# Twelve gate blocks as six pairs of seven block products ahead of the attention, six conv tiles in PSUM, squares of q and k in one operation

## The chip, the cores and the metric

The kernel runs on one core of one Trainium2 chip. The metric is the device time of one execution in microseconds. A core has TensorE (PE: matmuls, and PEld: the weight loads that run beside them), VectorE (DVE), ScalarE (ACT), GpSimd (POOL) and SyncE (SP, which issues most DMAs). TensorE writes to PSUM, the other engines read it from there.

## The reference

One layer of a decoder on x of 1024 tokens by 1024 channels, in float32:

```python
h = rms_norm(x, attn_norm_w[l])
proj = h @ w_in[l]
q, k, v, u, g = jnp.split(proj, splits, axis=-1)

q = rms_norm(q.reshape(B, S, N_HEADS, 2, HEAD_DIM), q_norm_w[l])
k = rms_norm(k.reshape(B, S, N_HEADS, 2, HEAD_DIM), k_norm_w[l])
...
a = diff_attention(q[0], q[1], k[0], k[1], v, lam, rel_bias)
a = rms_norm(a, subln_w[l]) * (1.0 - lam_init)
y_a = a.reshape(B, S, ATTN_WIDTH) @ w_proj_attn[l]

u_a, u_b = jnp.split(u, 2, axis=-1)
c = causal_depthwise_conv(u_a * jax.nn.sigmoid(u_b), conv_w[l], conv_b[l])
c = jax.nn.silu(layer_norm(c, conv_ln_w[l], conv_ln_b[l]))
y_b = c @ w_proj_conv[l]

g_a, g_b = jnp.split(jax.nn.sigmoid(g + gate_b[l]), 2, axis=-1)
x = x + (g_a * y_a + g_b * y_b) @ w_out[l]

h = rms_norm(x, ffn_norm_w[l])
gt, up = jnp.split(h @ w_gate_up[l], 2, axis=-1)
x = x + (jax.nn.silu(gt) * up) @ w_down[l]
```

`diff_attention` has 8 heads, each with two 64-wide parts of q and k, two causal softmaxes with a relative bias and a 128-wide v; its result is the first softmax minus lambda times the second, applied to v. The convolution is 31 wide over 1024 channels. g has 2048 columns (two gates).

## The kernel before

Every float32 product is made of three matmuls: each operand is split into a high part, rounded to a format that TensorE takes at full rate, and the low rest (`split_hi`, a cast on ScalarE, L120; `split_lo`, a subtraction on VectorE, L125, or on GpSimd, L131), and hi*hi, lo*hi and hi*lo are added (L168 to L170). h is kept transposed, `hT_hi` and `hT_lo`, for the whole input projection.

The output columns of that projection are made in items: V0 to V3 (256 columns of v), Q0 to Q7 (q and k of one head), U0 to U7 (a 128-channel tile of u) and G0 to G15 (a 128-column block of g). A G item (`g_item`) is two groups of 24 matmuls of 512 columns; each group ends in an ACT operation that adds the bias and a store to `g_d`. A Q item is four groups; ACT copies each group out of PSUM and squares it, eight operations with accumulated sums (L783).

U1 to U7 are made as pairs (`u_pair`): the two 128-column halves of a U item and the two halves of the tokens and of the channels form a two by two block product, and seven block products with sums of blocks take the place of eight. One block product is 12 matmuls of 512 columns (`product`, L963), so a pair has 84 where two plain blocks have 96. The sums of h's blocks (`TS`) are made once; those of the weights are made per pair by `prepare`, on GpSimd: four sums (L944 to L947) and the low parts of the splits (L131), while ScalarE makes the high parts. `ahead` is that generator for the next pair, advanced three times during a pair.

The order: an opening with V0 and U0; V1, V2 and the seven u pairs (to about 252 us in the profile); Q0 and V3; the attention, from about 310 to 823 us; the projection of its result (`w_proj_attn`) with the conv's layer norm (`ln_chunks`, `ln_step`) woven in; the conv's projection with the gates; w_out; and the feed-forward part, also by seven block products.

The conv is one DVE operation per tap (L582), 31 entries and a load for each of 8 channel tiles, in a list `bg` that is worked off beside other stages. The accumulators of the first `CONV_PSUM` tiles lie in PSUM and are finished in the first stage (`bg.until` at its end); the others are spread over the attention.

The attention has 64 steps: 8 heads by 8 blocks of 128 queries, `(h, i)`, in the order i = 4, 5, 6, 7, 0, 1, 2, 3 (6, 7, 4, 5, 2, 3, 0, 1 in the last head). A step makes the scores of both halves (`sc`; L1271, L1272) in pieces of up to 512 keys, each read by a DVE operation that adds the bias and keeps the minimum (L1273); ACT makes the exponentials (L1278), DVE combines both halves (L1288). One step later the result is transposed (`pT`, L1310) and split (`ph` by ACT, `pl` by DVE); after every second step it is multiplied with v (`pW`, `weigh`), and two steps later transposed back (`pB`, `back`). The finished head goes to `a_d` and is loaded again (`early`, L1468) and split into `aTh`, `aTl` for the projection.

Between these TensorE works off `fill`: the Q items of the next heads and all G items, in groups, one or none per step by `groups(n)`, and what is left after the last step. How many conv taps a step gets comes from `slack_of(n)`, an estimate of TensorE's and VectorE's time of the step in us.

All engines run their own instructions in order; which instruction stands where is set by the order of the code, by `after(...)` (an instruction is put behind a given one of another stream) and by a scheduler over them.

Of the kernel before, what the change touches and what calls it, by code (L numbers as in the profile page):

```python
# [16 lines left out]
P = 128  # L17
# [40 lines left out]
def kernel(  # L58
# [53 lines left out]
    def nm(s):  # L112
        uid[0] += 1
        return f"{s}_{uid[0]}"
# [9 lines left out]
    def split_lo(dst, src, hi):  # L124
        last_lo[0] = dve.tensor_tensor(dst, src, f32(hi), op=ALU.subtract).ins  # L125
# [244 lines left out]
    def gemm_N(o, halves, shi, slo, i):  # L370
# [24 lines left out]
    last = ["Q0", "V3"]  # L395
    later = [
        ["Q1", "G0", "G1"],
        ["Q2", "G2", "G3"],
        ["Q3", "G4"],
        ["Q4", "G5", "G6"],  # L400
        ["Q5", "G7"],
        ["Q6", "G8", "G9"],
        ["Q7", "G10"],
        ["G11", "G12", "G13", "G14"],
        ["G15"],
    ]

# [9 lines left out]

    for it in ["U0"] + first + last + [x_ for l_ in later for x_ in l_]:
        ws.plan(loads_of(it))
# [136 lines left out]
    us = {}  # L556
    CONV_PSUM = 4
    pcv = []
# [210 lines left out]
    def q_item(h):  # L769
# [3 lines left out]
        for b in (1, 0):  # L773
            raw = qkp.tile([P, 4, 256], F32, tag="qkraw", name=nm("qkraw"), bufs=2)
            ss = sm.tile([P, 16], F32, tag="ss16", name=nm("ss16"))
            for i2 in range(2):
                o = pg()
                for e in range(2):
                    gemm_N(o[:, 256 * e : 256 * (e + 1)], halves, hT_hi, hT_lo, 4 * b + 2 * i2 + e)
                act.copy(raw[:, 2 * i2 : 2 * i2 + 2, :], o[:].rearrange("p (e c) -> p e c", c=256))  # L780
                jk = sm.tile([P, VD], F32, tag="jk", name=nm("jk"), bufs=1)[:, :HD]
                for g in range(8):
                    act.activation(  # L783
                        jk, o[:, g * HD : (g + 1) * HD], AF.Square, accum_out=ss[:, 8 * i2 + g : 8 * i2 + g + 1]
                    )
                if i2 == 0:
                    yield
# [187 lines left out]
    def u_pair(c, A, ahead):  # L975
# [34 lines left out]
        return nxt  # L1010

    def first_stage():

# [3 lines left out]
        yield from opening()  # L1017
        ups = [prepare(win, (U0 + D + c * P, U0 + c * P), st[0], 2, c == 1) for c in range(1, NKT)]

        def weights_ahead():  # L1020
            yield
            ws.ahead = 1
            ws.fetch()
            yield

        for n, _ in enumerate(run(first)):
# [14 lines left out]
            yield  # L1041
        for c in range(1, NKT):
            ahead = ups[c] if c < NKT - 1 else weights_ahead()
            next(ahead)
            A = yield from u_pair(c, A, ahead)
        st_ctx.close()
# [472 lines left out]
    def ln_chunks(sb):  # L1519
# [15 lines left out]
        split_hi(s1h[:], s1[:])  # L1535
        split_lo(s1l[:], s1[:], s1h[:])
        for s_ in (s1h, s1l):
            pe.matmul(mean[:], part[:], s_[:], start=s_ is s1h, stop=s_ is s1l)
# [48 lines left out]

    def ln_step():
        for _ in range(lnp.pop(0)):
            next(lnq, None)  # L1590
# [31 lines left out]
    for c in range(NE):  # L1622
        ya_out(c, o3[c], g3[c])
    ln_step()
    for c in range(NE, NKT):
        w = ws.next()
        ln_step()
        ya_out(c, [gemm_T(w, aT_hi, aT_lo, sb) for sb in range(2)])
    while lnp:
# [362 lines left out]
```

## Time and profile before

| | before |
|---|---|
| median of 3 runs | 1743.23 us (1742.2 to 1744.04) |
| profiled execution | 1742.87 us, span 1741.1 us |
| TensorE, VectorE, ScalarE, GpSimd busy | 1728.2, 1249.4, 856.2, 210.9 us |
| mean granted TensorE clock | 0.999 |

A row of a group of instructions gives the line, the engine, the operation, output and inputs by the program's names, the shape, the count, and behind the bar the busy time in us, the mean of one in ns, the idle time of the engine just before them and what ended it. A row of the timeline gives start and length in us. Matmuls overlap in the records: the time from one start to the next is what one costs. A row of a stretch of time gives its bounds and length, then busy time and count of PE, PEld, DVE, ACT and POOL, the granted clock, the share of the DMA engines and GB/s. A row of DMA issues gives the size of one and the median time from issue to landing.

### The profile page before, as it was taken

To read this page: it belongs to the slowest core of one execution; us is meant where nothing else is said; L and a number is where in the kernel's file an instruction comes from. 1 tells how busy PE (TensorE), PEld (TensorE's weight loads), DVE (VectorE), ACT (ScalarE), POOL (GpSimd) and SP (SyncE) were. 2 spreads that over 40 slices of the span, in tenths; PEclk is the share of its full clock that TensorE was granted. 3 is DMA by queue.
4 is the path that set the end of the run, shared out by engine and by line. 5 is a ranking of instruction groups with operands and counts; after the bars stand their busy time and mean duration, and the time that the engine had idled before them with its cause. 6 is when DMAs were issued, how large, how long until landed. Compare 5 with 4: busy or idle time off the path is not lost.

```text
span 1741.1 us, 25854 instructions
## 1 busy us (share of the span) xinstructions
PE 1728.2 (99%) x9293; PEld 1488.6 (85%) x9293; DVE 1249.4 (72%) x2090; ACT 856.2 (49%) x1950; POOL 210.9 (12%) x199
## 2 busy tenths in 40 slices
PE   9999999999999999999999999999999999999999
PEld 7997889998998999988787888888888888888887
DVE  7575889898987988977787525876676666565554
ACT  5333435767776776756366313633333333333332
POOL 3997851000000000000000000000000000000000
PEclk9999999999999999999999999999999999999999
DMA  6343454234345244343863544235445444597663
GB/s 200 118 129 119 161 177 140 91 107 134 104 110 151 80 119 131 103 140 135 310 208 100 173 157 154 89 99 185 152 152 173 160 151 147 173 369 274 216 219 130
DMA packets 253253, 271.68 MB, mean 156 GB/s; under 512 B 15746, under 2 KB 177602, under 8 KB 253124
## 3 DMA queue, kind: packets, MB, share of 16 engines
q1 hardware_dynamic: 250848, 263.25, 46.7%
q0 software_dynamic: 1840, 5.19, 1.0%
q8 instruction: 73, 1.20, 0.3%
q10 hardware_dynamic: 436, 1.58, 0.2%
q14 instruction: 56, 0.46, 0.1%
HBM read 175.55 MB, written 78.16 MB: 146 GB/s over the span
## 4 chain that ended last, share of the span: by engine, by line
PE 91%; DVE 3%; DMA 2%; ACT 2%; POOL 1%; issue 1%; SPq 0%; POOLq 0%; DVEq 0%
PE acc L963 28%; PE acc L500 12%; PE pg L168 11%; PE pg L170 11%; PE pg L169 11%; PE sc L1272 2%; PE sc L1271 2%; PE pT L1310 2%; PE wo L170 2%; PE wo L169 2%; PE wo L168 2%; DVE acc L582 1%; PE pW L169 1%; PE pW L168 1%; PE pW L170 1%; PE pg L1089 1%
## 5 line engine op out<-in xcount | busy, mean ns | idle before, releaser
L582 DVE SCALAR_TENSOR_TENSOR acc<-u,cw,acc 128x1023 f32<-128x1023 f32 (+14 forms) x240 | 303.5, 1265 | 14.4 <-ACT acc L576 11.9
L168 PE MATMUL pg<-whi,hT_hi 128*128 128x256 f32 x704 | 200.2, 286 | 0.5 <-DVE v L125 0.5
L170 PE MATMUL pg<-whi,hT_lo 128*128 128x256 f32 x704 | 200.1, 285 | 0.0
L169 PE MATMUL pg<-wlo,hT_hi 128*128 128x256 f32 x704 | 199.7, 284 | 0.0
L120 ACT CAST whi<-wraw 128x1024 fp32r<-128x1024 f32 x100 | 105.0, 1052 | 126.4 <-PE wo L170 48.2
L125 DVE TENSOR_TENSOR wlo<-draw,whi 128x1024 fp32r<-128x1024 f32 x75 | 91.8, 1224 | 86.1 <-ACT whi L120 84.4
L125 DVE TENSOR_TENSOR wlo<-wraw,whi 128x1024 fp32r<-128x1024 f32 x85 | 104.9, 1236 | 56.5 <-ACT whi L120 55.9
L120 ACT CAST whi<-draw 128x1024 fp32r<-128x1024 f32 x75 | 79.0, 1053 | 129.6 <-PE acc L500 116.1
L168 PEld LDWEIGHTS pg<-whi,hT_hi 128*128 128x128 f32 x704 | 134.1, 191 | 2.2 <-DVE v L125 0.7
L169 PEld LDWEIGHTS pg<-wlo,hT_hi 128*128 128x128 f32 x704 | 134.4, 191 | 1.9
L170 PEld LDWEIGHTS pg<-whi,hT_lo 128*128 128x128 f32 x704 | 134.3, 191 | 1.7
L500 PE MATMUL acc<-wlo,whi 128*128 128x512 f32 x308 | 120.0, 390 | 0.0
L500 PE MATMUL acc<-whi,wlo 128*128 128x512 f32 x308 | 119.9, 389 | 0.0
L168 PE MATMUL pg<-hT_hi,whi 128*128 128x512 f32 x288 | 114.7, 398 | 0.1
L169 PE MATMUL pg<-hT_lo,whi 128*128 128x512 f32 x288 | 114.2, 397 | 0.0
L170 PE MATMUL pg<-hT_hi,wlo 128*128 128x512 f32 x288 | 113.8, 395 | 0.0
L1278 ACT ACTIVATE E<-E,mn 128x640 f32<-128x640 f32 (+7 forms) x128 | 99.7, 779 | 27.1 <-DVE mn L1273 26.4
L120 ACT CAST whi<-s 128x1024 fp32r<-128x1024 f32 x54 | 56.9, 1053 | 107.3 <-PE acc L963 103.5
L963 PE MATMUL acc<-h_hi,whi 128*128 128x512 f32 x240 | 93.5, 390 | 0.0
L963 PE MATMUL acc<-h_lo,whi 128*128 128x512 f32 x240 | 93.5, 390 | 0.0
L1273 DVE CUSTOM_DVE_ANT_0 E<-sc,tb 128x512 f32<-128x512 f32 (+3 forms) x128 | 74.1, 585 | 26.9 <-PE pT L1310 13.1
L963 PE MATMUL acc<-h_hi,wlo 128*128 128x512 f32 x240 | 90.2, 390 | 0.0
(337 smaller groups left out, 4554.9 us busy)
## 6 DMA issues: line engine op xcount, KB each, us to landing
wraw<-in_w_gate_up_dram SPq DMA_DIRECT2D x44, 512.0 KB, 4.9
wraw<-in_w_in_dram SPq DMA_DIRECT2D x40, 512.0 KB, 4.6
qs<-qs SPq DMA_DIRECT2D x96, 128.0 KB, 2.3
wd<-in_w_down_dram SPq DMA_DIRECT2D x44, 256.0 KB, 3.1
tdT<-wd SPq DMA_DIRECT2D x88, 128.0 KB, 4.7
draw<-sdS SPq DMA_DIRECT2D x44, 256.0 KB, 3.7
draw<-tdT SPq DMA_DIRECT2D x44, 256.0 KB, 4.0
wraw<-in_w_in_dram SPq DMA_DIRECT2D x32, 256.0 KB, 3.3
```

The costliest lines, as they stand in the source:

```text
L120: act.copy(dst, src)
L125: last_lo[0] = dve.tensor_tensor(dst, src, f32(hi), op=ALU.subtract).ins
L168: pe.matmul(o, lh, rh, start=start, stop=False)
L169: pe.matmul(o, lh, rl, start=False, stop=False)
L170: last_mm[0] = pe.matmul(o, ll, rh, start=False, stop=stop).ins
L500: m = pe.matmul(o[s_][i][:], l_[:, ts], r_[:, 512:], start=start and j + y_ == 0, stop=j == n - 1 and y_ == 2, skip_group_check=not start,)
L582: dve.scalar_tensor_tensor(a_, us[c][:, : S - n], cw[:, c, t : t + 1], a_, op0=ALU.mult, op1=ALU.add)
L963: last_mm[0] = pe.matmul(o[:], a_[x_][:, k, :], b_[y_][:, k, :], start=start and k + x_ + y_ == 0, stop=k == 3 and x_ == 1, skip_group_che ...
L1271: pe.matmul(o[:, :w], qh[:, qs], k, start=True, stop=False)
L1272: last_mm[0] = pe.matmul(o[:, :w], ql[:, qs], k, start=False, stop=True).ins
L1273: dve.tensor_tensor_reduce(e[:, ks], o[:, :w], tb[:, S - nk + c0 : S - nk + c0 + w], 1.0, mn[:, j : j + 1] if c0 else 3.0e38, ALU.add, ALU ...
L1278: act.activation(e[:, :nk], e[:, :nk], AF.Exp, bias=mn[:, j : j + 1], scale=-1.0, accum_out=l[:, j : j + 1])
```

## The change

- G0 to G11 are no longer items of `fill`. A new `g_pair` makes two neighbouring gate blocks by seven block products, in the first stage, behind the seven u pairs and prepared like them. Three of its four quarter results get their bias by a DVE operation with the other product (`add`), the fourth by ACT; each is stored to `g_d`.
- `fill` is Q1 to Q7, then G12 to G15: 36 groups in place of 60. Two of them are issued ahead of the first step, each with three entries of `bg`. Then `groups(n)` gives four per head (steps 0, 2, 5 and 7 of a head), and one per step in the last head.
- `CONV_PSUM` is 6: conv tiles 4 and 5 are also finished in the first stage.
- The squares of q and k: one ACT operation of 512 columns and one DVE reduce over groups of 64 take the place of eight ACT operations with sums.
- In the layer norm of the conv the two mean matmuls come one piece later (`yield`), the pieces are counted anew (`ln_both`, `lnp`), and the piece with the first mean is put inside the first group of the third projection block (`ln_amid`).

```diff
-    later = [
-        ["Q1", "G0", "G1"],
...
-        ["G11", "G12", "G13", "G14"],
-        ["G15"],
-    ]
+    NGP = 6
+    later = [f"Q{h}" for h in range(1, H)] + [f"G{c}" for c in range(2 * NGP, 2 * NKT)]
...
-    CONV_PSUM = 4
+    CONV_PSUM = 6
...
-                jk = sm.tile([P, VD], F32, tag="jk", name=nm("jk"), bufs=1)[:, :HD]
-                for g in range(8):
-                    act.activation(
-                        jk, o[:, g * HD : (g + 1) * HD], AF.Square, accum_out=ss[:, 8 * i2 + g : 8 * i2 + g + 1]
-                    )
+                sq = wp.tile([P, 512], F32, tag="sg", name=nm("qsq"), bufs=2)
+                act.activation(sq[:], o[:], AF.Square)
+                dve.tensor_reduce(
+                    ss[:, 8 * i2 : 8 * i2 + 8], sq[:].rearrange("p (g d) -> p g d", d=HD), axis=AX.X, op=ALU.add
+                )
...
+    def g_pair(c, A, ahead):
+
+        B = {(j, l): (hT_hi[:, KH[j], TOK[l]], hT_lo[:, KH[j], TOK[l]]) for j in range(2) for l in range(2)}
+        a, b, c_ = acc(), acc(), acc()
+
+        def add(d, o, l, t_):
+            dve.scalar_tensor_tensor(t_, o[:], pcol("gate_b", d), t_, op0=ALU.add, op1=ALU.add)
+            nc.sync.dma_start(g_d[d][:, TOK[l]], t_)
+
+        product(b, A["11"], B[0, 0], True)
+        p1 = half("p1")
+        act.copy(p1, b[:])
+        product(a, A["12"], B[1, 0], True)
+        add(c, a, 0, p1)
+        nxt = next(ahead, None)
+        yield
+        product(b, A["S2"], TS[2], False)
+        u2 = half("u2")
+        act.copy(u2, b[:])
+        product(c_, A["S1"], TS[1], True)
+        u3 = half("u3")
+        act.copy(u3, c_[:])
+        next(ahead, None)
+        yield
+        product(b, A["S3"], TS[3], False)
+        add(c + 1, b, 1, u3)
+        product(c_, A["S4"], B[1, 1], False)
+        add(c, c_, 1, u2)
+        yield
+        product(b, A["22"], TS[4], False)
+        p2 = half("p1")
+        act.activation(p2, b[:], AF.Identity, bias=pcol("gate_b", c + 1))
+        nc.sync.dma_start(g_d[c + 1][:, TOK[0]], p2)
+        next(ahead, None)
+        yield
+        return nxt
...
-        ups = [prepare(win, (U0 + D + c * P, U0 + c * P), st[0], 2, c == 1) for c in range(1, NKT)]
+        pairs = [(u_pair, c, (U0 + D + c * P, U0 + c * P)) for c in range(1, NKT)]
+        pairs += [(g_pair, 2 * c, (G0 + 2 * c * P, G0 + (2 * c + 1) * P)) for c in range(NGP)]
+        ups = [prepare(win, cols, st[0], 2, z == 0) for z, (_, _, cols) in enumerate(pairs)]
...
-    fill = run(it for l_ in later for it in l_)
-    plan = [sum(4 if it[0] == "Q" else 2 for it in l_) for l_ in later]
+    fill = run(later)
+    for _ in range(2):
+        next(fill)
+        with after(last_of(mybir.EngineType.DVE)):
+            bg.step(3)
...
-        return 0 if plan[n // NT] == 6 and n % NT in (4, 6) or n == len(steps) - 1 else 1
+        return int(n >= len(steps) - NT or n % NT in (0, 2, 5, 7))
...
-        for z in (0, 1, 0, 0, 0, 1, 1, 0, 0, 0, 1, 1, 1, 1):
+        for z in (0, 0, 1, 1, 0, 0, 0, 1, 1, 0, 0, 0, 1, 1, 1, 1):
...
-    lnp = [1, 3, 2, 2, 2, 2, 2, 9]
+    lnp = [1, 1, 4, 2, 2, 2, 2, 9]
...
+    def ln_amid():
+        with after(last_mm[0]):
+            ln_step()
+
     for c in range(NE, NKT):
         w = ws.next()
-        ln_step()
-        ya_out(c, [gemm_T(w, aT_hi, aT_lo, sb) for sb in range(2)])
+        if c > NE:
+            ln_step()
+        ya_out(c, [gemm_T(w, aT_hi, aT_lo, sb, ln_amid if c == NE and not sb else None) for sb in range(2)])
```

TensorE at the end of the attention, before: the last probabilities are transposed (`pT`), weighed (`pW`) and transposed back (`pB`), and a gate group (`pg<-hT`) stands between them and the projection (`pg<-aTh`):

```order
L1310 MATMUL pT_9727<-ident,E_9675 128x128 x2
L1330 MATMUL pB_9787<-ident,ar_9671 128x128 x2
L168 MATMUL pW_9795<-ph_9691,vh_9147 128x256
...
L170 MATMUL pW_9795<-ph_9691,vl_9148 128x256
L168 MATMUL pg_9853<-hT_hi,whi_9454 128x512
...
L1330 MATMUL pB_9820<-ident,ar_9802 128x128 x2
L168 MATMUL pg_9853<-hT_hi,whi_9454 128x512
L169 MATMUL pg_9853<-hT_lo,whi_9454 128x512
L170 MATMUL pg_9853<-hT_hi,wlo_9455 128x512
L168 MATMUL pg_9967<-aTh_9737,whi_9611 128x512
```

The same place after the change:

```order
L1340 MATMUL pT_9621<-ident,E_9553 128x128
L1340 MATMUL pT_9625<-ident,E_9601 128x128 x2
L1360 MATMUL pB_9651<-ident,ar_9597 128x128 x2
L168 MATMUL pW_9659<-ph_9617,vh_9112 128x256
...
L170 MATMUL pW_9659<-ph_9617,vl_9113 128x256
L1360 MATMUL pB_9684<-ident,ar_9666 128x128 x2
L168 MATMUL pg_9801<-aTh_9635,whi_9217 128x512
```

The gate group is gone from between `pW` and the projection; the last matmul on `hT` now stands ahead of the scores of step (7,2)'s second half.

TensorE in head 0 before, from the last score piece of step (0,7) to the first of (0,0): gate matmuls stand between the two.

```order
L1271 MATMUL sc_3521<-ks_0_1_2761,qs_0_1_2774 128x512
L1272 MATMUL sc_3521<-ks_0_1_2761,qs_0_1_2779 128x512
L170 MATMUL pg_3773<-hT_hi,wlo_3185 128x512
L168 MATMUL pg_3837<-hT_hi,whi_3190 128x512
...
L1271 MATMUL sc_3622<-ks_0_0_2940,qs_0_0_2953 128x128
L1272 MATMUL sc_3622<-ks_0_0_2940,qs_0_0_2956 128x128
```

After:

```order
L1301 MATMUL sc_4400<-ks_0_1_3604,qs_0_1_3617 128x512
L1302 MATMUL sc_4400<-ks_0_1_3604,qs_0_1_3622 128x512
L1301 MATMUL sc_4429<-ks_0_0_3771,qs_0_0_3784 128x128
L1302 MATMUL sc_4429<-ks_0_0_3771,qs_0_0_3787 128x128
L169 MATMUL pW_4361<-pl_4245,vh_3980 128x256
```

The scores of (0,0) follow those of (0,7) directly, with the weighing behind them in place of a gate group.

VectorE in head 0 after the change, between two score pieces of step (0,7) and the next ones: conv taps (`acc<-u,cw,acc`) stand between the attention's own operations as before the change.

```order
L1303 ISA E_4395,mn_4383<-sc_4400,tb_3398,mn_4383 128x512
L1303 ISA mn_4383 128x1
L573 SCALAR_TENSOR_TENSOR acc_3474<-u_3090,cw,acc_3474 128x1002
L630 TENSOR_SCALAR t_4341<-t_4341 128x16
L1303 ISA E_4428,mn_4426<-sc_4429,tb_3398 128x128
L1303 ISA mn_4426 128x1
L573 SCALAR_TENSOR_TENSOR acc_3474<-u_3090,cw,acc_3474 128x1001
L1315 RECIPROCAL rl_0_4145<-l_4384 128x2
```

By this order head 0 has 21 taps where 20 stood, and each of the next six heads 3 or 4 where 12 to 15 stood, with four reduces (`ss16<-qsq`) in most of them.

More of the change, by code (lines that the diff above doesn't have):

```diff
@@ L395 @@
     last = ["Q0", "V3"]
-    later = [
-        ["Q1", "G0", "G1"],
[L398 to L403, printed above, removed]
-        ["G11", "G12", "G13", "G14"],
-        ["G15"],
-    ]
+    NGP = 6
+    later = [f"Q{h}" for h in range(1, H)] + [f"G{c}" for c in range(2 * NGP, 2 * NKT)]
     def loads_of(it):
@@ L416, in loads_of @@
         return ld_cols(win, G0 + c * P)
-    for it in ["U0"] + first + last + [x_ for l_ in later for x_ in l_]:
+    for it in ["U0"] + first + last + later:
         ws.plan(loads_of(it))
@@ L1041, in first_stage @@
             yield
-        for c in range(1, NKT):
-            ahead = ups[c] if c < NKT - 1 else weights_ahead()
+        for z, (make, c, _) in enumerate(pairs):
+            ahead = ups[z + 1] if z + 1 < len(pairs) else weights_ahead()
             next(ahead)
-            A = yield from u_pair(c, A, ahead)
+            A = yield from make(c, A, ahead)
         st_ctx.close()
@@ L1536, in ln_chunks @@
         split_lo(s1l[:], s1[:], s1h[:])
+        yield
         for s_ in (s1h, s1l):
```

1 line of the change is left out of this document (removed).

## The prediction

> **What bounds the kernel now.** I read the page's busy shares first, then the chain that ended last, then the attention head by head.
>
> ```profile
> PE 1728.2 (99%) x9293; PEld 1488.6 (85%) x9293; DVE 1249.4 (72%) x2090; ACT 856.2 (49%) x1950; POOL 210.9 (12%) x199
> ...
> PE 91%; DVE 3%; DMA 2%; ACT 2%; POOL 1%; issue 1%; SPq 0%; POOLq 0%; DVEq 0%
> ```
>
> TensorE is busy 99% of the span and is 91% of the chain: fewer matmuls shorten the kernel, as long as no other engine makes TensorE wait. The view by stretches of time asks who could: one row per head, then the tail of attention.
>
> ```profile
> 310.10:375.20 65.10, 65.10 (x436) 59.96 (x436) 60.35 (x124) 42.97 (x140) 0.73 (x4) 1.00 0.28 82
> 375.20:440.80 65.60, 65.48 (x440) 59.71 (x439) 57.09 (x128) 49.57 (x167) 1.44 (x8) 1.00 0.45 129
> 440.80:501.20 60.40, 60.40 (x444) 57.24 (x443) 52.56 (x124) 45.44 (x155) 1.45 (x8) 1.00 0.37 106
> 501.20:565.90 64.70, 64.57 (x430) 58.76 (x429) 52.98 (x122) 47.29 (x153) 1.80 (x10) 1.00 0.45 130
> 565.90:627.60 61.70, 61.48 (x453) 58.22 (x452) 54.44 (x124) 45.19 (x166) 1.09 (x6) 1.00 0.37 104
> 627.60:691.40 63.80, 63.80 (x427) 58.28 (x426) 56.91 (x126) 46.56 (x157) 1.69 (x10) 1.00 0.43 124
> 691.40:754.20 62.80, 62.80 (x416) 57.31 (x416) 53.25 (x122) 47.03 (x160) 1.20 (x7) 1.00 0.37 106
> 754.20:802.80 48.60, 48.60 (x279) 42.15 (x278) 42.66 (x95) 29.48 (x74) 1.45 (x8) 1.00 0.38 114
> 802.80:822.70 19.90, 19.62 (x100) 16.18 (x99) 12.79 (x22) 12.96 (x35) 0.36 (x2) 1.00 0.60 211
> ```
>
> The columns after the length are busy time (and count) of TensorE, its weight loads, VectorE, ScalarE and GpSimd. TensorE never waits, but VectorE has 60.35 us of work in a head of 65.10, and 53 to 57 in the next ones. What separates the two is the gate matmuls that the change takes out.
>
> **The change part by part.** Durations, from the groups and the timeline:
>
> ```profile
> L582 DVE SCALAR_TENSOR_TENSOR acc<-u,cw,acc 128x1023 f32<-128x1023 f32 (+14 forms) x240 | 303.5, 1265 | 14.4 <-ACT acc L576 11.9
> ```
>
> ```profile
> L168 PE MATMUL pg<-hT_hi,whi 128*128 128x512 f32 x248 | 98.7, 398 | 0.1
> L1273 DVE CUSTOM_DVE_ANT_0 E<-sc,tb 128x512 f32<-128x512 f32 x80 | 54.4, 685 | 21.3 <-PE sc L1272 8.6 <-PE pT L1310 8.3 <-PE pg L170 3.4
> L783 ACT ACTIVATE jk<-pg 128x64 f32<-128x64 f32 x224 | 50.5, 225 | 5.0
> L783 ACT ACTIVATION_READ_ACCUMULATOR jk<-pg 128x1 f32 x224 | 44.7, 199 | 0.0
> L125 DVE TENSOR_TENSOR wlo<-wraw,whi 128x1024 fp32r<-128x1024 f32 x30 | 36.5, 1220 | 2.4 <-ACT whi L120 1.8 <-PE pg L170 0.5
> L790 DVE TENSOR_TENSOR qkraw<-qkraw,r 128x1024 f32<-128x1024 f32 x14 | 17.0, 1218 | 0.0
> ```
>
> ```profile
> 228.76 0.39 PE L963 MATMUL acc<-T3h,whi 128*128 128x512 f32 x1
> ...
> 231.49 0.39 PE L963 MATMUL acc<-hT_hi,wlo 128*128 128x512 f32 x1
> ```
>
> Twelve 512-column matmuls lie between the two starts, so one costs (231.49 - 228.76)/12 = 0.227 us of TensorE.
>
> *Matmuls.* Twelve gate blocks of 48 matmuls become six pairs of 84: 576 - 504 = 72 fewer, 72 x 0.227 = 16.3 us gained, whatever else happens. Six pairs add 6 x 84 x 0.227 = 114.4 us to the first stage, and 576 x 0.227 = 130.8 us leave the attention.
>
> *Preparing the pairs.* A pair costs TensorE 19.1 us. GpSimd has to keep up, by these rows of the seven u pairs:
>
> ```profile
> L131 POOL TENSOR_TENSOR wlo<-s,whi 128x1024 fp32r<-128x1024 f32 x14 | 33.7, 2408 | 9.7 <-ACT whi L120 9.6
> L131 POOL TENSOR_TENSOR wlo<-wraw,whi 128x1024 fp32r<-128x1024 f32 x10 | 24.1, 2409 | 8.3 <-DMA wraw<-in_w_in_dram 4.4 <-ACT whi L120 3.8
> L947 POOL TENSOR_TENSOR s<-wraw,s 128x512 f32<-128x512 f32 x7 | 9.1, 1298 | 0.1
> L944 POOL TENSOR_TENSOR s<-wraw 128x512 f32<-128x512 f32 x7 | 9.1, 1294 | 15.0 <-DMA wraw<-in_w_in_dram 14.9
> L131 POOL TENSOR_TENSOR sl<-wraw,sh 128x512 fp32r<-128x512 f32 x7 | 9.1, 1293 | 1.4 <-ACT sh L120 1.4
> ```
>
> ```profile
> wraw<-in_w_in_dram SPq DMA_DIRECT2D x14, 512.0 KB, 4.7
> ```
>
> Three splits, four sums and the small split are 3 x 2.41 + 4 x 1.30 + 1.29 = 13.7 us, and with the whole 4.7 us of the load 18.4, under 19.1; a u pair carries one multiply more and TensorE did not wait for it. VectorE has three 0.69 us adds in a pair and up to 11 taps of 1.2 us: within 19.1. SP issues two loads and four stores of 256 KB a pair, where a u pair has two loads, two stores and a reload of u;
>
> ```profile
> 94.00:252.00 158.00, 157.89 (x773) 131.32 (x772) 115.86 (x109) 59.71 (x80) 122.57 (x82) 1.00 0.42 137
> ```
>
> the DMA engines were 0.42 busy in the u pairs (the last column but one), which leaves room for 0.5 MB more in 19 us. I take 0.5 us for the stage; the ends are 0 and, if each pair's load took 4 us longer than 4.7, 6 x 3.3 = 20.
>
> *Squares.* Eight squares with their read-outs, 8 x (0.225 + 0.199) = 3.4 us of ScalarE, become one operation and a reduce on VectorE. The trace has no such reduce; the nearest row is the 512-wide reduce of the scores, 0.685 us. With 28 of them VectorE gets 19 us more inside the attention, four per head. I count 0.69 each (0.5 to 1.0); ScalarE is at 43 to 50 of 60 us, so its gain moves nothing. The Trainium skill ("VectorE: DVE Perf Modes", Rules for kernel authors) tells one to expect the slowest rate of `tensor_reduce` and to restructure it away from a hot path; it speaks against this edit. At half the rate I assume the reduces would add another 19 us of VectorE, three a head, and the sum below would be some 3 us higher in head 0; no run so far shows the operation.
>
> *A head from the second on.* Three gate groups of 24 x 0.227 = 5.4 us leave it on average (8 or 6 groups become 4): TensorE 63 - 16 = 47 us. VectorE loses ten taps (12.6 us) and 1.5 weight splits (1.8) and gets four reduces (2.8): 54.5 - 11.6 = 43. Slack shrinks from about 8 us to 4. I take 2 us of new waits over six heads; ends 0 and 6.
>
> *Head 0.* It keeps 21 taps (20 before) and loses gate matmuls. By the order after the change, from the last score piece of step (0,5) to the transposes of (0,7), TensorE has 140 matmuls of 256 columns, 12 of 512, 6 of 384 and 21 short ones. A 256-column one is 0.12 us, by these rows:
>
> ```profile
> 816.48 0.28 PE L170 MATMUL pW<-ph,vl 128*128 128x256 f32 x1
> ...
> 816.84 0.28 PE L170 MATMUL pW<-ph,vl 128*128 128x256 f32 x1
> ```
>
> That is 16.8 + 2.7 + 1.1 + 21 x 0.11 = 22.9 us. VectorE between the same points has 9 taps (11.4), 2 weight splits (2.4), 2 normalisations (2.4), 10 score reduces (6), 6 low halves (3.3), 3 combines (3.3), the new reduce and a turn (1.4) and some 25 small ones (2.8): 33 us of durations, 29 with their overlap of some tenth taken off (taps start 1.2 apart and last 1.26). It falls 6 to 10 us behind here; (0,7)'s transposes need its last combine, so TensorE waits. The same count over the head of the order before falls 7 us behind, and TensorE was busy for 65.10 of 65.10 us, so a lag of some size is free; now the fall from (0,5) to (0,2) is 16. Between 16 - 7 = 9 and the 6 of the shorter stretch I take 7 (ends 2, if buffers carry more than the 7 seen, and 10).
>
> *Tail.* Before, the last four and a half gate groups stand between the small steps of head 7 and the projection; the fill now ends in step (7,5). From the low half of (7,5)'s probabilities, TensorE has 36 matmuls of 256 columns and some 20 short ones left: 7 us. VectorE from there has three taps and the rest of the steps: 10 us to the last low half, and 9 to the combine of (7,0), which frees the buffer for `early0`. Then:
>
> ```profile
> early<-a_d SPq DMA_DIRECT2D x5, 512.0 KB, 5.0
> ```
>
> ```profile
> 817.15 0.37 ACT L1324 COPY ar<-pW 128x256 f32<-128x256 f32 x1
> 817.42 2.00 ACT L120 CAST aTh<-early 128x1024 fp32r<-128x1024 f32 x2
> ```
>
> Load 5.0, cast 1.05 (two in 2.00): the projection's first matmul can start 9 + 0.3 + 5.0 + 1.05 = 15.4 us after that point, 8.4 later than TensorE is done, plus what VectorE lags there already (1 to 3). I take 10; ends 5 (no lag, a tap fewer, a faster load) and 15. Before, the load was hidden behind gate groups.
>
> *Clock after the tail.* The trace shows one stall of that kind, in the projection:
>
> ```profile
> 845.90:850.00 4.10, 0.97 (x2) 0.37 (x2) 3.64 (x5) 4.07 (x6) 0.00 (x0) 0.94 0.40 121
> 850.00:853.40 3.40, 3.33 (x9) 2.67 (x10) 3.40 (x7) 1.48 (x3) 0.00 (x0) 0.57 0.96 313
> ```
>
> After 4.1 us with two matmuls the granted clock fell to 0.57 for 3.4 us; nine matmuls ran where 15 fit: 6 x 0.227 = 1.4 us lost. I add that once (ends 0 and 2.8). The Trainium skill ("TensorE: Matmul & The Clock Gate", Part 1: The HAM clock gate) has the clock halved after an idle window of about 3.4 us until one such window is busy again; the trace agrees (3.4 us at 0.57). By that rule a tail of waits each under 3.4 us would cost no clock, and the sum would be 1.4 less.
>
> *Norm.* The first mean now sits inside the next GEMM:
>
> ```profile
> 845.31 0.39 PE L170 MATMUL pg<-aTh,wlo 128*128 128x512 f32 x1
> 847.49 0.47 PE L1538 MATMUL mean<-lnmh,part 128*128 128x512 f32 x1 [1.79 <-ACT lnmh L120]
> 848.93 0.50 PE L1538 MATMUL mean<-lnml,part 128*128 128x512 f32 x1 [0.97 <-DVE lnml L125]
> 850.07 0.79 PE L168 MATMUL pg<-aTh,whi 128*128 128x512 f32 x1 [0.63 <-DVE gt L1607]
> ```
>
> The GEMM still waits for the gate multiply that frees its PSUM tile, behind the same casts and table load, so only the two means' time goes: -0.5 (ends -2.5 and 0).
>
> *Sum:* -16.3 + 0.5 + 2 + 7 + 10 + 1.4 - 0.5 = +4.1 us. Against the profiled execution, 1742.87 us (span 1741.1), that is 1747.0; this execution lies 0.36 under the median of 1743.23, so **1747.3 us**. 0.2% (3.5 us) is about what a measurement tells from no change.
>
> **Rivals.** *Faster: the waits are short.* If buffers carry more of VectorE's lag than the 7 us that head 0 showed, head 0 costs 2, the other heads 0, the tail 5 with no clock loss: -16.3 + 0.5 + 2 + 5 - 0.5 = -9.3, **1734**. It decides where the new waits stay under 12.8 us together. For it: 99% busy with VectorE at 93% of head 0. Against: the tail's load has no cover at all.
>
> *No change.* Tail 8, head 0 5, 2 elsewhere: -16.3 + 15 + 1.4 = 0, **1743**.
>
> *Slower by the preparation.* If the loads of 512 KB come as late as the heads' DMA makes them elsewhere, GpSimd's 13.7 us begin late in each pair and TensorE waits 2 to 3 us six times: 4.1 + 15 = **1762**. Against it: seven u pairs without such a wait.
>
> *How the numbers follow.* Forecast (slower, 1746.8 to 1756) 0.42; faster 0.38, since the gain is sure and each wait is estimated; no change 0.14; preparation 0.06. Faster 0.38, same 0.14, slower 0.48. The low end, 1732, is new waits of 5 us in all, less than the faster rival counts; the upper ends of head 0, the heads, the tail and the clock together give -16.3 + 0.5 + 10 + 6 + 15 + 2.8 = +18, of which I keep 14: 1757. The preparation and the two tails beyond stay outside.
>
> **What would show it.** Right: `g_pair` products at 0.227 us without gaps; a TensorE wait of 5 us or more released by VectorE's combine around steps (0,6) to (0,2); no matmul on `hT` after (7,5), then waits ending in ScalarE's `aTh` cast of about 10 us, and a stretch near 0.5 clock in the projection. Wrong: heads of 44 to 48 us with TensorE at 100%, or gaps in the first stage with GpSimd as releaser.

## The result and the profile after

The changed kernel takes 1768.69 us (median of 4 runs, 1766.56 to 1771.82) against 1742.8 us: 1.0149 times as long, 95% interval 1.0131 to 1.0168. The direction is that of the forecast, the size is not: +26 us in place of +4, and outside the range. Its profiled execution has a span of 1765.4 us, 24.3 more than before.

The page of the changed kernel, busy shares and the chain that ended last:

```profile
PE 1726.2 (98%) x9221; PEld 1478.6 (84%) x9221; DVE 1275.9 (72%) x2128; ACT 810.3 (46%) x1484; POOL 292.3 (17%) x247
...
PE 82%; DVE 10%; DMA 3%; ACT 3%; issue 2%; SPq 0%; DVEq 0%; ACTq 0%
```

TensorE ran the 72 matmuls less (9221 against 9293), and yet its share of the chain fell from 91% to 82%; VectorE's rose from 3% to 10%. The matmuls went, and waits on VectorE came. Where, the view by stretches shows, one row per head (heads 0 to 7 by their first score, then from the last step's scores to the projection):

```profile
413.80:482.90 69.10, 63.60 (x472) 60.06 (x473) 68.25 (x138) 34.84 (x85) 2.07 (x5) 0.95 0.29 84
482.90:532.20 49.30, 46.54 (x355) 43.10 (x354) 44.59 (x120) 35.85 (x92) 1.46 (x8) 1.00 0.42 118
532.20:582.00 49.80, 48.77 (x382) 46.23 (x382) 43.59 (x116) 37.16 (x102) 1.49 (x8) 1.00 0.39 106
582.00:632.90 50.90, 47.66 (x373) 45.27 (x372) 44.53 (x117) 36.04 (x96) 1.44 (x8) 1.00 0.38 105
632.90:680.90 48.00, 46.27 (x357) 43.56 (x356) 42.77 (x116) 34.72 (x91) 1.45 (x8) 1.00 0.39 110
680.90:732.30 51.40, 49.35 (x371) 46.43 (x370) 43.74 (x117) 36.45 (x98) 1.45 (x8) 0.97 0.38 104
732.30:789.20 56.90, 56.90 (x347) 50.15 (x346) 42.41 (x108) 38.22 (x96) 1.44 (x8) 1.00 0.40 113
789.20:832.80 43.60, 39.94 (x238) 34.02 (x236) 36.37 (x88) 28.81 (x74) 1.45 (x8) 1.00 0.41 126
832.80:844.10 11.30, 6.83 (x34) 5.00 (x32) 6.84 (x20) 7.25 (x27) 0.41 (x2) 0.85 0.52 172
```

Before, TensorE filled nearly all of each such row. Now head 0 has VectorE busy for 68.25 of 69.10 us and TensorE waiting for 5.5, and most heads behind it have waits though VectorE has 5 to 8 us to spare.

A busy time hides a part of such losses, since a matmul that waits is longer in the records than one in a row (at 718.16 us below, 0.50 us against 0.40 for the next one of the same width). So I count the loss otherwise: the time from each matmul's start to the next one's, less what that width costs in a row (0.2265 us for 512 columns, 0.175 for 384, 0.1195 for 256, 0.11 for 128). The sum of these prices is 1706.7 us before and 1690.4 after, 16.3 less, and what lies above it is this excess, in us:

| stretch | before | after | more |
|---|---|---|---|
| opening and first stage, to the first score | 15.0 | 14.1 | -0.9 |
| head 0 | 0.3 | 10.2 | 9.9 |
| heads 1 to 6 | 3.0 | 20.4 | 17.4 |
| head 7 to the last step's scores | 0.5 | 5.5 | 5.0 |
| from there to the projection | 1.1 | 7.7 | 6.6 |
| projection to w_out, with the norm | 7.6 | 10.6 | 3.0 |
| the rest | 1.1 | 1.1 | 0 |
| sum | 28.8 | 69.5 | 40.7 |

The rows are rounded each for itself. -16.3 + 40.7 = 24.4, the difference of the spans (24.3). In heads 1 to 6 after the change the excess is 4.9, 2.2, 4.4, 3.3, 5.1 and 0.5, head by head, and 12.6 of it lies in the last steps (i = 3) of heads 1 to 5.

The gate pairs themselves cost what was forecast. From 149.5 us, in the u pairs, to 353.1, in the last gate pair of the changed kernel:

```profile
149.50:353.10 203.60, 203.60 (x899) 168.38 (x898) 174.81 (x158) 75.30 (x99) 153.90 (x98) 1.00 0.42 139
```

TensorE is busy throughout, at 203.60/899 = 0.2265 us a matmul; GpSimd (153.90) and the DMA engines (0.42) keep up.

The end of head 5 shows what a wait of the later heads looks like, on TensorE in the changed kernel:

```profile
718.16 0.50 PE L1301 MATMUL sc<-ks,qs 128*128 128x512 f32 x1
718.50 0.40 PE L1302 MATMUL sc<-ks,qs 128*128 128x512 f32 x1
719.19 0.63 PE L789 MATMUL pQ<-ident,qkraw 128*128 128x128 f32 x4 [0.30 <-DVE pl L125]
720.18 0.63 PE L789 MATMUL pQ<-ident,qkraw 128*128 128x128 f32 x4 [0.36 <-DVE pl L125]
721.70 0.33 PE L1340 MATMUL pT<-ident,E 128*128 128x128 f32 x1 [0.89 <-DVE qs L798]
721.88 0.41 PE L168 MATMUL pg<-whi,hT_hi 128*128 128x256 f32 x1
```

Scores, two sets of transposes of q and k (`pQ`), then transposes of probabilities (`pT`): each stands behind a VectorE eviction (`pl`, `qs`) of one of the PSUM tiles that these operations share, and no matmul group stands between. The group comes at 721.88, behind the waits, and until 725.3 it runs at 0.21 us a matmul from start to start in place of 0.12. By what was waited for, the five largest in heads 1 to 6 of the changed kernel (total us, times, longest), together 9.9 us of the 20.4:

```profile
PE pT L1340 <- DVE qs L798: 2.7, 3, 0.9
PE pQ L789 <- DVE pl L125: 2.7, 7, 0.7
PE sc L1301 <- DVE mn L1303: 2.4, 3, 1.5
PE pW L168 <- ACT jk L1369: 1.1, 2, 0.6
PE pW L168 <- DVE pl L125: 1.0, 2, 0.5
```

Many small waits, none over 1.5 us. And the tail of the changed kernel, on TensorE, with ScalarE's first cast for the projection:

```profile
833.83 0.27 PE L1340 MATMUL pT<-ident,E 128*128 128x128 f32 x1
835.51 0.39 PE L168 MATMUL pW<-ph,vh 128*128 128x256 f32 x1 [1.41 <-ACT ph L120]
837.80 0.39 PE L169 MATMUL pW<-pl,vh 128*128 128x256 f32 x1 [1.91 <-DVE pl L125]
...
843.12 0.44 PE L1360 MATMUL pB<-ident,ar 128*128 128x128 f32 x2 [0.46 <-ACT ar L1354]
844.07 0.73 PE L168 MATMUL pg<-aTh,whi 128*128 128x512 f32 x2 [0.50 <-ACT aTh L120]
```

```profile
842.97 1.05 ACT L120 CAST aTh<-early 128x1024 fp32r<-128x1024 f32 x1
```

The granted clock (the last column but two) falls in three stretches in which it did not before, here each with the 3.4 to 4.1 us ahead of it:

```profile
449.10:452.50 3.40, 1.14 (x8) 0.83 (x7) 3.40 (x7) 1.97 (x5) 0.00 (x0) 0.99 0.61 189
452.50:459.20 6.70, 5.58 (x24) 5.04 (x23) 6.70 (x17) 2.37 (x4) 0.04 (x1) 0.50 0.00 0
718.70:722.10 3.40, 1.85 (x11) 1.19 (x11) 2.80 (x7) 3.40 (x13) 0.00 (x0) 1.00 0.08 29
722.10:725.50 3.40, 3.40 (x17) 3.40 (x17) 3.33 (x10) 3.25 (x10) 0.00 (x0) 0.50 0.71 168
834.00:838.10 4.10, 0.78 (x4) 0.48 (x4) 4.10 (x12) 2.55 (x10) 0.00 (x0) 1.00 0.04 15
838.10:841.60 3.50, 3.50 (x17) 2.93 (x15) 1.34 (x5) 1.08 (x4) 0.41 (x2) 0.51 0.97 318
```

### The profile page after: what moved, and what is told of

Its sections match the earlier page's. It is cut to its first block, busy times and chain, and to the rows that moved or that the text cites. A ratio compares the mean times of both kernels' runs of the same rounds, so it can differ in the third digit from the quotient of the medians.

```text
span 1765.4 us, 25407 instructions
## 1 busy us (share of the span) xinstructions
PE 1726.2 (98%) x9221; PEld 1478.6 (84%) x9221; DVE 1275.9 (72%) x2128; ACT 810.3 (46%) x1484; POOL 292.3 (17%) x247
## 4 chain that ended last, share of the span: by engine, by line
PE 82%; DVE 10%; DMA 3%; ACT 3%; issue 2%; SPq 0%; DVEq 0%; ACTq 0%
PE acc L954 36%; PE acc L491 12%; PE pg L168 7%; PE pg L169 7%; PE pg L170 7%; DVE acc L573 2%; PE wo L168 2%; PE wo L170 2%; PE wo L169 2%; DVE E L1303 1%; DMA gt<-g_d 1%; PE sc L1302 1%; PE sc L1301 1%; PE pT L1340 1%; PE pg L1119 1%
## 5 line engine op out<-in xcount | busy, mean ns | idle before, releaser
L120 ACT CAST whi<-wraw 128x1024 fp32r<-128x1024 f32 x94 | 98.9, 1054 | 121.8 <-PE wo L170 48.1
L120 ACT CAST whi<-s 128x1024 fp32r<-128x1024 f32 x66 | 69.5, 1053 | 143.2 <-PE acc L954 137.4
L125 DVE TENSOR_TENSOR wlo<-wraw,whi 128x1024 fp32r<-128x1024 f32 x73 | 90.4, 1240 | 59.9 <-ACT whi L120 59.7
L491 PE MATMUL acc<-whi 128*128 128x512 f32 x308 | 84.6, 389 | 0.0
L1301 PE MATMUL sc<-ks,qs 128*128 128x512 f32 (+2 forms) x192 | 70.8, 372 | 6.2 <-DVE mn L1303 6.0
L1331 POOL MEMSET pl<- 128x128 f32 x32 | 6.6, 207 | 413.9 <-PE pW L169 347.4
```

The source lines that it names most:

```text
L120: act.copy(dst, src)
L491: m = pe.matmul(o[s_][i][:], l_[:, ts], r_[:, 512:], start=start and j + y_ == 0, stop=j == n - 1 and y_ == 2, skip_group_check=not start,)
L1301: pe.matmul(o[:, :w], qh[:, qs], k, start=True, stop=False)
```

## The experiments

Theory A: the waits are VectorE's load (new reduces, taps, in heads that became shorter). Theory B: they are single chains of short matmuls and evictions in stretches where no matmul group stands. The ratios are to the kernel before; "head n" is the excess of that head as in the table above.

**The squares back on ScalarE.** Label `e1_old_squares`.

```diff
-                sq = wp.tile([P, 512], F32, tag="sg", name=nm("qsq"), bufs=2)
-                act.activation(sq[:], o[:], AF.Square)
-                dve.tensor_reduce(...)
+                jk = sm.tile([P, VD], F32, tag="jk", name=nm("jk"), bufs=1)[:, :HD]
+                for g in range(8):
+                    act.activation(jk, o[:, g * HD : (g + 1) * HD], AF.Square, accum_out=...)
```

> The changed kernel with the eight squares per group put back on ScalarE, all else as changed. Theory A (TensorE's waits in the attention are VectorE's load: 28 new reduces of about 0.69 us each are 19 us): the time falls by 10 to 18 us, to 1751 to 1759. Theory B (the waits are single chains of transposes and evictions that stand in steps without a matmul group; the load of one engine is not what ends last): it falls by 5 us at most, or rises, since a group costs ScalarE 3.4 us again, which does evictions in the same chains: 1764 to 1772.

Measured: 1787.66 us, 1.0251 (1.0236 to 1.0266), 19 us more than the changed kernel. Heads 1 to 6 go from 20.4 to 34.9 us of excess. In heads 1 to 6 TensorE now waits for ScalarE, for the squares themselves too (`jk`, L774):

```profile
PE pg L168 <- ACT jk L774: 4.4, 4, 1.4
PE pW L168 <- ACT jk L1369: 3.9, 5, 1.8
PE pQ L789 <- DVE pl L125: 3.8, 5, 1.5
PE pW L168 <- ACT ph L120: 3.2, 2, 1.6
```

Taking 19 us from VectorE made it worse, but the same edit gives ScalarE 51 us more (861.7 in place of 810.3), so this run alone does not refute A. By the waits, what the squares hold up is the PSUM tile and the evictions queued behind them. The time lies outside the ranges of both theories.

**No taps in the attention.** Label `e2_no_taps`; the conv of tiles 6 and 7 is left out but for two taps each.

```diff
             def go():
                 n = CW - 1 - t
                 a_ = acc[0][:, n:]
+                if c >= CONV_PSUM and t:
+                    return
```

> The changed kernel without the taps of conv tiles 6 and 7 after their first and last (58 VectorE operations of 1.2 us left out of the attention). Theory A: head 0's waits of about 9 us and most of the 23 us in the later heads go: 1736 to 1745. Theory B: head 0's 9 us go, the later heads keep at least 15 of their 23, the tail (three taps fewer) loses 2 to 4: 1753 to 1758.

Measured: 1752.92 us, 1.0049 (1.0032 to 1.0066). Head 0's 10.2 us are gone (0.1). Heads 1 to 6 have 20.5 (20.4 with the taps), head 7 and the tail 10.1 (13.2). Head 2 here:

```profile
519.00:567.30 48.30, 47.40 (x373) 45.42 (x372) 40.00 (x112) 34.59 (x90) 1.50 (x8) 1.00 0.40 110
```

So head 0 needs the taps to wait, and the later heads' sum is not the taps: as B has it. Their waits also change releaser here (a DMA of `ks` 2.3 us, one of `vl` 1.1), so the chain that ends last is not one particular one.

**Only the squares changed, in the kernel before.** Label `e3_before_squares`.

> The kernel before with only the squares changed (one operation on ScalarE and a reduce on VectorE). Theory A: VectorE goes from 53 to 60 us of a head's 60 to 65 to 56 to 63, so some waits come: 1745 to 1750. Theory B: the gate groups cover them: 1742 to 1745.

Measured: 1753.97 us, 1.0057 (1.0042 to 1.0072), slower by 10 us: neither theory had so much. 3.9 us of excess are in head 2, 5.5 in head 7 up to its last scores, and the projection has 12.1 in place of 7.6. The waits:

```profile
PE sc L1271 <- DVE mn L1273: 3.7, 5, 1.1
PE pg L168 <- ACT cT_hi L120: 3.6, 2, 1.8
...
PE pT L1310 <- DVE rl L1285: 1.5, 1, 1.5
```

With 120 of the conv's 240 taps still in the attention (55 in the changed kernel), VectorE's reduces do hold up the scores; the 3.6 us at the conv's projection (`cT_hi`) come in a stage that this edit does not touch, and why they come is open. The same edit is worth 19 us in the changed kernel and costs 10 in the one before.

**Five pairs, and the tail covered.** Label `e4_ngp5_tail`.

```diff
-    NGP = 6
+    NGP = 5
...
-        return int(n >= len(steps) - NT or n % NT in (0, 2, 5, 7))
+        return int(n != len(steps) - 1 and (n >= len(steps) - NT or n % NT in (0, 2, 5, 7)))
```

> Five gate pairs in place of six; the four groups more are used in the last head (one per step but the last) and behind it, so that the tail is covered as before the change. Costs 12 matmuls, 2.7 us. If the tail cost about 10 us as forecast (the excess of 820 to 860 us in the trace is 10.8 against 1.4): 1758 to 1763. If the loads of the finished heads bound it in any case: 1770 to 1772.

Measured: 1768.93 us, 1.014 (1.0124 to 1.0155), the same as the changed kernel. The cover does its work: head 7 and the tail go from 13.2 us of excess to 1.4. But head 0 goes from 10.2 to 15.3 and heads 1 to 6 from 20.4 to 26.7, so with the 2.7 us of matmuls nothing is left, and the time lies in neither range. Head 0 has fewer taps here than in the changed kernel (20 in place of 25) and waits more; what it also has less of is matmuls on `hT` (218 in place of 337). VectorE is busy there for 57.14 of 60.00 us:

```profile
408.40:468.40 60.00, 51.39 (x356) 47.95 (x355) 57.14 (x122) 32.20 (x76) 0.71 (x4) 0.89 0.16 41
```

**The same groups in other steps.** Label `e5_two_at_end`.

```diff
-        return int(n >= len(steps) - NT or n % NT in (0, 2, 5, 7))
+        return int(n >= len(steps) - NT) or (0, 0, 1, 0, 0, 1, 0, 2)[n % NT]
```

> The changed kernel with the same 36 groups in other steps: two in the last step of each of heads 0 to 6 (i = 3, where 12.6 us of the waits of heads 1 to 5 lie), one at i = 6 and one at i = 1, none at i = 4. Theory B (a step without matmuls between its transposes shows the latency of their evictions): the waits at i = 3 fall from 12.6 to under 5 us, and if the other steps stand without the group, the time falls by 5 to 9 us to 1760 to 1764. If the amount of cover per head counts and not its place, the waits move to i = 4 to 7 and the time stays within 2 us of 1768.7 or rises.

Measured: 1792.76 us, 1.028 (1.0263 to 1.0298), 24 us worse than the changed kernel with the same work. Excess comes at i = 4 to 6 of heads 1 to 6 (3.8 to 5.3 us together in each), where at i = 4 and 5 no fill matmul is left, and at i = 3 it did not fall (1.8 to 5.0 in heads 1 to 5). So the place of a group counts very much, but two groups given to a step do not stand between its transposes by that: the order is the scheduler's. My expectation for i = 3 failed.

**A group issued between the transposes.** Label `e13_between`: the group of the first step of heads 1 to 6 is called inside `slot`, behind the first `turn_qk`.

```diff
                 if late[0][0] <= n:
                     late.pop(0)[1]()
+                    if n % NT == 0 and 0 < n < len(steps) - NT and between.count(n) == 0:
+                        between.append(n)
+                        group()
```

> The changed kernel with the same 36 groups, of which the one that stood in the first step of heads 1 to 6 is issued between the transposes of q and k of that step instead of ahead of them. Theory B says the waits around the turn of a head (12.6 us in heads 1 to 5, up to 2.6 each) are evictions of transposes with nothing between; they fall to under 6 us, and the time by 4 to 8 us to 1761 to 1765. If the order of these rows does not matter: 1767 to 1771.

Measured: 1798.01 us, 1.0311 (1.0292 to 1.033): a miss. In the order that results the last step of heads 1 to 5 has 1 to 9 fill matmuls where the changed kernel has 46 to 59, and 4.3 to 8.7 us of excess there in place of 1.4 to 4.1. The run does not test what it was meant to, and shows the same thing from the other side for this step: without a group the turn of a head costs more. It is no rule for every step: at i = 0 the same heads have 5 to 11 fill matmuls and no excess.

**The old norm order.** Label `e8_old_norm`: `ln_both`, `lnp` and the place of the first mean as before.

> The changed kernel with the norm's pieces in the old order. The forecast had 0.5 us for this edit: 1769 to 1770. The excess from the projection to w_out is 10.6 us after against 7.6 before; if the edit makes this rise, the time falls by 2 to 3 us to 1766.

Measured: 1768.28 us, 1.0145 (1.013 to 1.016), not to be told from the changed kernel. Excess from the projection on 11.3 in place of 10.6: by that the edit is worth its half microsecond, which the times cannot show, and the 3 us more than before in that stretch are not from it.

**Two pairs.** Label `e7_two_pairs`, the way to something faster: two gate pairs, five conv tiles, old squares and norm, six groups in heads 0 to 6.

```diff
+    NGP = 2
+    later = [it for h in range(1, H) for it in (f"Q{h}", f"G{2 * NGP + h - 1}")]
+    later += [f"G{c}" for c in range(2 * NGP + H - 1, 2 * NKT)]
...
+    CONV_PSUM = 5
...
+        return int(n != len(steps) - 1 and (n >= len(steps) - NT or n % NT not in (4, 6)))
```

> The kernel before with two gate pairs instead of six, five conv tiles in PSUM, the old squares and the old norm, six groups in each of heads 0 to 6, seven in the last and three behind it. 24 matmuls fewer, 5.4 us. Theory B (cover counts): most of it stays, 1737 to 1742. Theory A (VectorE's load counts, which is 53 to 57 us a head with one tap fewer in six): the same or 1741 to 1746. If any move of gate blocks costs more than it saves: over 1746.

Measured: 1749.68 us, 1.0033 (1.002 to 1.0046). Heads 1 to 6 have 1.8 us of excess together, head 7 and the tail 1.5: as before the change. All of the loss is in head 0, 13.3 us, so theory B's 1737 to 1742 failed there and held in the later heads. The rows of heads 0 and 1:

```profile
354.90:414.30 59.40, 51.71 (x324) 46.25 (x323) 55.51 (x115) 36.66 (x112) 0.77 (x4) 0.91 0.26 76
414.30:471.60 57.30, 57.28 (x416) 54.13 (x417) 49.24 (x119) 44.40 (x153) 1.44 (x8) 1.00 0.38 106
```

**Three pairs.** Label `e10_three_pairs_h0`: as that, three pairs, heads 0 to 4 with six groups, 5 and 6 with four, and no share of taps for head 0.

> Three gate pairs: 36 matmuls fewer than before, 8.2 us; heads 0 to 4 with six groups, heads 5 and 6 with four, the last as before. Theory B (from six groups to four the cover breaks): heads 0 to 4 within 1 us of their matmuls' time, heads 5 and 6 with 3 to 6 us of waits each: 1738 to 1745. If four groups are enough with the old squares, five conv tiles and an even share of taps: no waits in heads 5 and 6 and 1734 to 1737.

Measured: 1759.87 us, 1.0089 (1.0074 to 1.0103), slower than both ranges. It has both amounts of cover in one kernel: heads 0 to 3 have 0.1 to 1.8 us of excess, heads 4 to 6 have 7.0, 7.1 and 3.4, in their last steps above all (3.8 and 5.5 in heads 4 and 5, where no fill matmul stands). By the plan head 4 has six groups too; in the order that results it has 192 fill matmuls, as head 5, against 242 in head 2. Head 6 does not fit: it has 216, many of them 512 wide, and still 3.4. Heads 2 and 5:

```profile
482.20:539.70 57.50, 57.50 (x420) 54.32 (x419) 49.44 (x120) 46.14 (x161) 1.45 (x8) 1.00 0.43 122
651.30:704.30 53.00, 49.91 (x365) 47.46 (x366) 43.35 (x114) 43.58 (x155) 1.14 (x6) 0.94 0.41 112
```

Head 5 has 6 us less of VectorE than head 2, and it is head 5 that waits.

**Head 0 of the two pairs.** Four kernels tried to keep the 5.4 us of matmuls: `e9_two_pairs_h0` (no share of taps for head 0), `e12_two_pairs_8` (eight groups in head 0, four in head 6), `e14_ahead` and `e15_gates_first` (eight in head 0, one behind the last step).

```diff
     slack[-2:] = [0.0, 0.0]
+    slack[:NT] = [0.0] * NT
```

> Two gate pairs as before, with the share of conv taps for head 0 set to nothing (11 taps stand there in place of 19; the others move to later heads, one or two each). With 19 taps head 0 had 13.3 us more than its matmuls take and every other head 0.5 or less. If VectorE's lag in head 0 is the cause: 1736 to 1739, faster than the kernel before. If six groups do not cover head 0 in any case: 1744 to 1750. If the later heads now stall with two more taps: 1740 to 1744.

> Two gate pairs, old squares, old norm, five conv tiles; head 0 gets eight groups in place of six, heads 1 to 5 six, head 6 four, the last as before. If VectorE's taps in head 0 need as much cover as before the change: head 0's 13.3 us go, head 6 costs 0 to 4: 1736 to 1742, faster than before. If head 0's waits come from something else (its taps stand in front, whatever the share says): 1747 to 1753.

> Two gate pairs, old squares and norm, five conv tiles, items in the order Q1, G4, Q2, G5 and so on; eight groups in head 0, six in heads 1 to 6, seven in the last and one behind it. If the waits are where a stretch has no matmul group (head 0 with six groups 13.3 us, heads with four up to 7, heads with six at most 0.5): no waits in heads 0 to 6, the tail 2 to 4 us longer for its two missing groups, 1737 to 1742. If taking 5.4 us of matmuls from the attention always brings a wait elsewhere: 1744 to 1750.

> The same with two gate blocks behind Q1 and then Q2, one gate block and so on, as the kernel before has it. As the run beside it; if the place of the squares of Q2 at the start of head 1 costs what it did with the other arrangement (5.9 us in head 1): 1743 to 1748.

| | time, us | ratio (95%) | head 0 | head 1 | heads 2 to 6 | head 7 and tail |
|---|---|---|---|---|---|---|
| two pairs | 1749.68 | 1.0033 (1.002 to 1.0046) | 13.3 | 0.2 | 1.6 | 1.5 |
| e9 | 1752.55 | 1.0046 (1.0033 to 1.006) | 13.7 | 0.3 | 3.4 | 2.6 |
| e12 | 1749.45 | 1.0035 (1.0021 to 1.0048) | 0.6 | 5.9 | 8.6 | 1.6 |
| e14 | 1760.57 | 1.0098 (1.0084 to 1.0112) | 3.6 | 12.9 | 4.3 | 4.8 |
| e15 | 1750.61 | 1.0046 (1.0032 to 1.0059) | 0.6 | 5.5 | 5.3 | 4.7 |

Eight groups cover head 0 in e12 and e15 (0.6, with the 19 or 20 taps that wait under six groups), less so in e14 (3.6). The share of taps does nothing for it: the 11 taps that are left in e9 stand at the same places as the first 11 of the two pairs, up to 389 us. But what head 0 gains comes back in head 1 and behind, and why head 1 waits there with about six groups beside it is open. e9, e14 and e15 miss all of their ranges; e12 has the time of its second case and the head 0 of its first. None of the four is faster than the kernel before.

**Holding those taps back.** Labels `e16_two_pairs_hold` and `e17_hold` (the changed kernel).

```diff
         with after(last_of(mybir.EngineType.DVE)):
-            bg.step(int(due))
+            if n < 28 or len(bg.todo) > (NKT - CONV_PSUM) * (CW + 1):
+                bg.step(int(due))
```

> Two gate pairs with six groups per head, as the run with 13.3 us of excess in head 0, but no tap of the tiles left for the attention is issued in the last part of the first stage: 7 taps in head 0 in place of 19, 11 or 12 in each later head in place of 9 to 11. If the taps queued ahead of head 0's own VectorE work are the cause there: head 0 within 2 us, 1736 to 1741, faster than before. If head 0 with six groups waits in any case: 1746 to 1752.

> The changed kernel with the same hold: 8 taps in head 0 in place of 24, 4 to 8 in each later head in place of 3 or 4. Head 0's excess of 10.2 us goes to 2 or less if the taps are its cause. If the later heads' waits are chains with no group between (theory B), they stay at 22 to 28 us and the time is 1759 to 1762; if they are VectorE's load (theory A), they rise by as much as head 0 gains, 1767 to 1771.

Measured: 1764.69 us, 1.0117 (1.01 to 1.0134), and 1773.53 us, 1.0172 (1.0157 to 1.0187). The first does not answer its question: the hold also kept back taps that have to be done before the attention, and TensorE waited 16.6 us for the last of them ahead of the first score. Head 0 fell to 4.0. The second does: with 8 taps in head 0 in place of 24 or 25 its excess is 1.3 in place of 10.2, VectorE 48.16 of 59.60 us:

```profile
416.10:475.70 59.60, 59.09 (x467) 57.31 (x468) 48.16 (x119) 33.03 (x82) 0.71 (x4) 1.00 0.29 81
```

Heads 1 to 6 rise from 20.4 to 25.6, head 7 and the tail from 13.2 to 18.3, and the whole is 5 us slower. Theory B's number for the whole (1759 to 1762) fails, and the time is above theory A's too (1767 to 1771): some 20 taps more do add 10 us in heads that already wait, as A has it, though taking all taps away there takes nothing. The taps are not what makes those waits, but more of them lengthen them.

## Why the prediction was right and wrong

- *Matmuls, -16.3 us:* right, by the prices of all matmuls 1706.7 to 1690.4.
- *Preparing the pairs, 0.5:* right. No wait in the first stage.
- *Squares:* the reduce takes what was assumed, 0.683 us (row below, in the attention of the changed kernel), so the doubled price did not come. The claim that ScalarE's gain moves nothing was wrong: undoing the edit costs 19 us. I had read ScalarE's sum (43 to 50 of 60 us) and not its place, ahead of the evictions for which TensorE waits.

```profile
L774 DVE TENSOR_REDUCE ss<-qsq 128x8 f32<-128x512 f32 x28 | 19.0, 683 | 0.9 <-ACT qsq L773 0.7
```

- *Head 0, 7 (2 to 10):* right in that VectorE falls behind, 9.9 in size. Without taps 0.1, with taps held back 1.3; by the trace 25 taps start in head 0, where 22 did before and the order was read as 21. The sign, one wait of 5 us or more for the combine, did not come: the longest is 1.8. Up to 3.4 of the 9.9 are the lowered clock (half of the 6.7 us from 452.5), which the forecast had as another term, so that the size fits is in part luck. The two pairs show that the cover counts here too: two groups more take 13.3 to 0.6 with 19 or 20 taps (e12, e15).
- *A head from the second on, 2 (0 to 6):* this is the step that failed. The loads that it worked out came true, TensorE 47 and VectorE 43 forecast, 46.5 and 44.6 in head 1. What was wrong is what followed from them, that 4 us of slack in the sums leave 2 us of waits in six heads. Measured 17.4 in heads 1 to 6 (the 5.0 of head 7 are counted with the tail). A head is not one queue: its last steps are chains of short matmuls and evictions, and before the change a group of 24 matmuls stood nearly everywhere beside them. From six groups a head to four that cover breaks (with three pairs 0.1 to 1.8 us of excess in heads 0 to 3, 7.0 and 7.1 in heads 4 and 5), with VectorE less loaded. Head 6 of the changed kernel agrees: its order has some six groups' worth of matmuls on `hT` (33 us, against 21 to 24 in heads 1 to 5), and it has 0.5. In all 17 traces, heads 1 to 5: the 43 with four groups' worth or little more (3.9 to 4.7) all have 1.6 us or more; of the 42 with 5.7 or more, 34 have at most 1.1, the other 8 from 1.9 to 12.9 (a group's worth is 24 x 0.2265 = 5.44 us). So too little cover has always cost, and enough of it has not always been enough.
- *Tail, 10 (5 to 15):* right in size, only in part in its path. 6.6 behind the last scores and 5.0 in head 7 ahead of them; covering it removes 11.8 (13.2 to 1.4). The load was not alone in it: the longest waits are for the last halves of the probabilities (1.91 and 1.41), the cast at 842.97 did not wait for its load, and the wait that ends in it is 0.50 where about 10 was the sign. VectorE's own order is in those waits: the `pl` that ends the 1.91 runs behind a conv tap (835.91, 1.24 us), and without taps head 7 and the tail have 3.1 less. The loads come out close behind, as forecast: the second is issued at 839.38, behind the combine, and ScalarE starts its cast at 844.36 after waiting for it.
- *Clock, 1.4 once:* too small. There are three new stretches at half clock; (1 - clock) times their length is 6.8 us at most (3.4 in head 0, 1.7 in head 5, 1.7 in the tail), part of it in idle time, and it is contained in the excess of those rows. The rule of the Trainium skill ("TensorE: Matmul & The Clock Gate", Part 1: The HAM clock gate) has the clock halved after an idle window of about 3.4 us. I drew from it that a tail of waits each under 3.4 us would cost no clock, and the traces do not bear that out: from 448.71 to 452.5 us the longest gap from start to start is 2.2 us, and the clock is at 0.50 behind it. The rows of the stall in the prediction show it too, with no gap over 2.2 (845.31 to 847.49).
- *Norm, -0.5:* right for the edit (0.7 less excess than with the old order); that stretch still has 3.0 more than before, which is not explained.
- *Rivals:* the preparation's rival gave 1762, near the measured time, for a cause that did not occur. The faster one said that the waits would stay under 12.8 us; they are 40.7.

Of the 20.3 us between the forecast's +4.1 and the 24.4 of the profiles, 15.4 are heads 1 to 6, 2.9 head 0, 3.5 the norm's stretch, 0.2 the tail with head 7 and the clock; the first stage gave 1.4 back (each rounded for itself). That waits of the later heads follow from the lack of cover is shown by the runs with two and three pairs and by the count over all traces; which chain ends last in each step is not settled, since the order of the engines changed in every run. No run changes the six conv tiles or the two groups ahead of the first step alone, so their part is open.

## What to carry to other kernels

Matmuls that fill a latency-bound loop are worth more there than their own time: a cheaper form of them in another stage has to be charged with every wait that they covered. Here 16.3 us were saved and 40.7 came, with the taps of head 0 and the lowered clock in it; heads 1 to 6 alone took 17.4. Slack in sums over a stage says that an engine can keep up, not that nobody waits; look at the places without filler, and ask whose eviction frees the PSUM tile of the next short matmul. Where a scheduler sets the order, moving one group moves many rows, so the cover has to be read from the order and not from the plan.

## What the runs showed of the hardware that I had not expected

- The clock fell after short waits that add up: in the 3.4 us before it went to 0.50, TensorE was busy for 1.14 us in head 0 and for 1.85 in head 5, with no gap from start to start over 2.2 us. It stayed there for 6.7 and 3.4 us.
- A 512-wide reduce of float32 in groups of 64 takes VectorE 683 ns, the same as a 512-wide subtraction of two tensors (`pl`, 684).
